# Layer 1's feed-forward block: the second product in smaller groups, five of eight row pairs by seven products, and two gate panels made as one double panel

## The chip, the cores and the metric

The kernel runs on one core of a Trainium2 chip. Its engines work side by side: TensorE (PE in the rows; PEld is its weight load) multiplies matrices, VectorE (DVE) and ScalarE (ACT) work element by element, GpSimd (POOL) does little here, and SyncE (SP) issues most transfers. Each engine takes its instructions in the order in which the program lists them for it. The metric is the time of one execution in microseconds (us) of device time, as the median of several runs.

## What is computed

Two layers in sequence on 256 tokens of width 2048, all in float32. Layer 1 is a mixer of two attentions with sigmoid gates, a cross attention to a memory, and a SwiGLU block; layer 2 is another gated mixer. Cut to what the change touches:

```python
def hybrid_mixer(x, ...):                       # layer 1
    o_a = dsa_attention(...)                    # 8 heads of 128
    o_b = moba_attention(...)                   # 8 heads of 128, causal with distance slopes at S = 256
    g_a = jax.nn.sigmoid(ga + b_gate[0])        # ga, gb: columns of x @ w_in
    g_b = jax.nn.sigmoid(gb + b_gate[1])
    merged = g_a * (o_a @ w_o_dsa) + g_b * (o_b @ w_o_moba)
    return merged @ w_out

def swiglu(x, w_in, w_out):                     # D_FF = 5632
    g, u = jnp.split(x @ w_in, 2, axis=-1)
    return (jax.nn.silu(g) * u) @ w_out

x = layer_norm(ALPHA * x + swiglu(x, w_ffn_in, w_ffn_out), ln_g[2], ln_b[2])
```

## The kernel before

**Products.** To keep float32 accuracy each operand is split into a rounded part `hi` (ScalarE, L107) and a remainder `lo` (VectorE, L108), and each product of two operands takes three matmuls: hi with hi, lo with hi, hi with lo (`mm3`, `mm3s`). The weights are the moving operand, 512 columns to a matmul. Weights come by DMA into `raw` tiles of 128x1024, which hold two blocks of 128 rows; there are six buffers each for `raw`, `hi` and `lo` (N_R, N_W). The 256 tokens are two halves, `tt` 0 and 1.

**Panels.** `gemm_panels` makes products of one panel (512 output columns) after another: per block of 128 rows 2 halves x 3 = 6 matmuls into two `ps_g` banks of PSUM. There are four `ps_g` banks and four `ps_m` banks.

**Double panels.** `duo` makes two panels together. It goes through the 16 row blocks in eight pairs. A pair in `eight` takes 2 blocks x 2 panels x 6 = 24 matmuls. A pair in `seven` takes seven block products of 3 matmuls in place of eight, 21 in all (Strassen's scheme in a variant): VectorE forms four sums of weight blocks (L255 one of 128x1024, L257 and L261 of 128x512 each), and these are split like weights, three tiles of 128x1024 and one of 128x512 in place of two tiles. L261 forms the last half of the tile that is split right after it. Sums of activations for a pair (`sums_of`) are made once per activation and kept. Four of the seven results gather in the four `ps_m` banks (`N`) over all pairs by seven; behind the last of them `combine` (L297 to L301) reads the banks, and the banks are free again. At the end `finish` (L305) adds each `ps_g` bank to the combined part, for (half, panel) in the order (0,0), (0,1), (1,0), (1,1). PLAN = (0, 3, 1, 4, 2, 5, 6, 7) is the order of the pairs, FAST = (0, 1, 2) those by seven.

**Queues of work.** `later_q` holds transposes of finished results, which `flush()` runs in the middle of a later product; `idle_q` holds small work of VectorE, of which `spare()` runs one piece between blocks. A scheduler then lists each engine's instructions in an order of its own within what the data allow.

**Around the change.** In the mixer, `ob = alibi_attention(...)` goes through four pairs of heads. For each, TensorE makes scores (L372), VectorE and ScalarE make the softmax, TensorE transposes the probabilities (L395, L396, L399), ScalarE copies them (L405), and TensorE weighs the values (L406, L407), all through `ps_m` banks. Next in the program stand the gate panels `ga[0]` and `ga[1]`, each a `gemm` of its own through `ps_g`, 96 matmuls each. Behind them stands `gate_pair` for `gb[0]`, `gb[1]`, a double panel.

In the feed-forward block `ffn_in(j)`, j = 0 to 10, makes 512 columns of g and of u (j = 0 as two single panels, the others as a double panel), `ev_g` applies silu, `ev_u` multiplies (L843), and `to_pair` transposes the result into `hT[j]` later. FFN_GROUPS cuts the second product: three `ffn_in` and the first of the next group, then four panels over 12 row blocks (288 matmuls); the last group has 8 row blocks. `residual` adds each panel of the second product to x (L721, L723).

Of the kernel before, what the change touches and what calls it, by code (L numbers as in the profile page):

```python
# [28 lines left out]
TAIL = 8  # L29
# [6 lines left out]
FAST2 = (0, 1)  # L36

FFN_GROUPS = ((0, 3), (3, 6), (6, 9), (9, 11))
# [6 lines left out]
def build(ctx, tc, nc, a):  # L45
# [167 lines left out]
    def duo(w0, w1, evacs, acts, sums, plan=PLAN, dest=None):  # L213
# [96 lines left out]
        rest, flushed = list(plan), False  # L310
        while rest:
            i = rest.pop(0)
            if i in sums:
                seven(i)
                if i == fast[-1]:
                    combine()
                    flush()
                    flushed = True
            elif len(rest) <= 1:
                eight([i] + rest)  # L320
                rest = []
            else:
                eight([i])
                if not fast and not flushed:
                    flush()
                    flushed = True
        return
# [350 lines left out]
    ga = {}  # L678
    ga[0] = gate_panel(a["w_ga"][0], xA, cols(0, 0), "ga")
    ga[1] = gate_panel(a["w_ga"][1], xA, cols(0, 1), "ga")  # L680
    gb = {}
# [149 lines left out]
    def ffn_in(j):  # L831
# [8 lines left out]
        hT[j] = pair("hT")  # L840

        def ev_u(tt, ps):
            nc.vector.tensor_mul(sg[tt], sg[tt], ps)  # L843
            later_q.append(lambda: to_pair(sg[tt], hT[j], tt))

        if j == 0:
            idle_q.extend(sums_later(x2S, x2T) + ln_affine(1))
            gemm(a["w_fi"][0], x2A, ev_g, head=HEAD)
            gemm(a["w_fi"][1], x2A, ev_u)
            spare(-1)  # L850
        else:
            duo(a["w_fi"][2 * j], a["w_fi"][2 * j + 1], (ev_g, ev_u), x2A, x2S, PLAN)
# [6 lines left out]

    groups = [range(j0, j1) for j0, j1 in FFN_GROUPS]  # L860
    for gi, g in enumerate(groups):
        for j in g:
            if j not in hT:
                ffn_in(j)
        last = gi == len(groups) - 1
        if not last:
            ffn_in(groups[gi + 1][0])
        flush()
        acts = acts_of([hT[q] for q in g])
        if last:  # L870
            hnT = [pair("hnT") for _ in range(4)]
            ln = layer_norm_T(g3[:, 0, :], g3[:, 1, :], hnT, None)
        gemm_panels([(a[f"w_fo{gi}"][j], acts, residual(j, gi == 0, last, ln)) for j in range(4)], tail=TAIL if last else 0)
# [349 lines left out]
```

## Time and profile before

| what | value |
|---|---|
| median of 3 runs | 2188.13 us (2187.45 to 2192.49) |
| the profiled execution | 2189.2 us |
| its span, first to last instruction | 2187.5 us |
| TensorE busy | 2163.9 us, 99% |
| VectorE busy | 1684.9 us, 77% |
| ScalarE busy | 1173.6 us, 54% |
| DMA | 426.10 MB, mean 195 GB/s |
| mean granted clock of TensorE | 0.999 |

Matmuls overlap in the pipeline, so that the time from one start to the next is their price, not the duration shown. The same holds for VectorE: the next instruction starts a little before the end that is shown.

### The profile page before, as it was taken

Reading aid. Unit: us, or ns where it says so; the run is one execution under the profiler, and the core shown is the slowest. Engines: PE = TensorE matmul, PEld = TensorE weight load, DVE = VectorE, ACT = ScalarE, POOL = GpSimd, SP = SyncE. Lnnn points to the kernel's source line nnn. Section 1 sums busy time; section 2 is a strip of 40 time slices with the busy share of each in tenths; the row PEclk is TensorE's granted clock in tenths of the full one; section 3 lists DMA queues with packets and bytes.
Section 4 is the critical chain, followed back from the end, with each engine's and each line's share of the span. In section 5 each row is a group of like instructions: output and inputs, shape, how many; then the busy total and the mean of one; then the engine's idle time right before and its main releaser. Section 6 shows DMA issues by size and latency. Waiting matters only on the chain.

```text
span 2187.5 us, 27170 instructions
## 1 busy us (share of the span) xinstructions
PE 2163.9 (99%) x9873; PEld 1780.2 (81%) x9873; DVE 1684.9 (77%) x2184; ACT 1173.6 (54%) x1494; POOL 43.2 (2%) x87
## 2 busy tenths in 40 slices
PE   8999999999999999999999999999999999999999
PEld 6888888888888788888888888877788787888887
DVE  5688877888767799858967886778676778998784
ACT  5665554455456555545544554547565656554542
POOL 1000000000000000000000000001000000000000
PEclk9999999999999999999999999999999999999999
DMA  7544646568666466655665665556645455665753
GB/s 280 180 154 136 225 135 206 183 202 270 207 206 212 140 202 216 207 190 174 198 227 170 204 208 185 202 182 227 208 158 179 162 193 178 220 204 182 247 201 129
DMA packets 138934, 426.10 MB, mean 195 GB/s; under 512 B 16000, under 2 KB 16560, under 8 KB 138800
## 3 DMA queue, kind: packets, MB, share of 16 engines
q1 hardware_dynamic: 132480, 403.40, 56.0%
q0 software_dynamic: 6320, 20.97, 3.0%
q8 instruction: 77, 1.26, 0.2%
q14 instruction: 57, 0.47, 0.1%
HBM read 420.11 MB, written 4.19 MB: 194 GB/s over the span
## 4 chain that ended last, share of the span: by engine, by line
PE 75%; issue 10%; DVE 8%; DMA 5%; ACT 2%; SPq 0%; POOL 0%; ACTq 0%; DVEq 0%; POOLq 0%
PE ps_g L132 11%; PE ps_g L131 11%; PE ps_g L130 11%; PE ps_g L211 10%; PE ps_g L210 10%; PE ps_g L209 10%; DVE lo L108 4%; PE ps_m L209 2%; PE ps_m L210 2%; PE ps_m L211 2%; DMA raw<-w_fi 1%; PE ps_t L339 1%; ACT hi L107 1%; DMA raw<-w_out 1%; DMA raw<-w_qkvg 1%
## 5 line engine op out<-in xcount | busy, mean ns | idle before, releaser
L107 ACT CAST hi<-raw 128x1024 fp32r<-128x1024 f32 (+1 forms) x904 | 905.4, 1016 | 864.5 <-PE ps_g L132 351.3
L108 DVE TENSOR_TENSOR lo<-raw,hi 128x1024 fp32r<-128x1024 f32 (+1 forms) x904 | 1048.2, 1174 | 362.6 <-ACT hi L107 354.9
L211 PE MATMUL ps_g<-hi,x2Tl 128*128 128x512 f32 x460 | 179.8, 391 | 0.0
L209 PE MATMUL ps_g<-hi,x2Th 128*128 128x512 f32 x460 | 179.8, 391 | 0.0
L210 PE MATMUL ps_g<-lo,x2Th 128*128 128x512 f32 x460 | 179.1, 389 | 0.0
L130 PE MATMUL ps_g<-hi,hTh 128*128 128x512 f32 x352 | 137.6, 391 | 0.0
L132 PE MATMUL ps_g<-hi,hTl 128*128 128x512 f32 x352 | 137.2, 390 | 0.0
L131 PE MATMUL ps_g<-lo,hTh 128*128 128x512 f32 x352 | 137.0, 389 | 0.0
L209 PE MATMUL ps_g<-hi,hnTh 128*128 128x512 f32 x334 | 130.4, 391 | 0.0
L211 PE MATMUL ps_g<-hi,hnTl 128*128 128x512 f32 x334 | 130.4, 390 | 0.0
L210 PE MATMUL ps_g<-lo,hnTh 128*128 128x512 f32 x334 | 130.4, 390 | 0.0
L132 PE MATMUL ps_g<-hi,hnTl 128*128 128x512 f32 x320 | 125.6, 393 | 1.3 <-DVE hnTl L759 1.3
L130 PE MATMUL ps_g<-hi,hnTh 128*128 128x512 f32 x320 | 126.4, 395 | 0.0
L131 PE MATMUL ps_g<-lo,hnTh 128*128 128x512 f32 x320 | 125.3, 391 | 1.0 <-DVE lo L108 1.0
L130 PE MATMUL ps_g<-hi,xTh 128*128 128x512 f32 (+1 forms) x288 | 114.1, 396 | 6.6 <-ACT hi L107 6.5
L255 DVE TENSOR_TENSOR raw<-raw 128x1024 f32<-128x1024 f32 x69 | 84.2, 1221 | 42.8 <-DMA raw<-w_qkvg 11.7
L131 PE MATMUL ps_g<-lo,xTh 128*128 128x512 f32 (+1 forms) x288 | 112.4, 390 | 0.8 <-DVE lo L108 0.8
L132 PE MATMUL ps_g<-hi,xTl 128*128 128x512 f32 (+1 forms) x288 | 112.7, 391 | 0.0
L211 PEld LDWEIGHTS ps_g<-hi,x2Tl 128*128 128x128 f32 x460 | 86.4, 188 | 18.0
L209 PEld LDWEIGHTS ps_g<-hi,x2Th 128*128 128x128 f32 x460 | 86.3, 188 | 17.7
L210 PEld LDWEIGHTS ps_g<-lo,x2Th 128*128 128x128 f32 x460 | 86.4, 188 | 17.6
L209 PE MATMUL ps_g<-hi,xTh 128*128 128x512 f32 x230 | 89.9, 391 | 0.0
(446 smaller groups left out, 4067.5 us busy)
## 6 DMA issues: line engine op xcount, KB each, us to landing
raw<-w_fi SPq DMA_DIRECT2D x116, 512.0 KB, 4.8
raw<-w_fo SPq DMA_DIRECT2D x88, 512.0 KB, 4.8
raw<-w_qkvg SPq DMA_DIRECT2D x82, 512.0 KB, 4.8
raw<-w_g SPq DMA_DIRECT2D x72, 512.0 KB, 4.9
raw<-w_fi SPq DMA_DIRECT2D x120, 256.0 KB, 4.0
raw<-w_out SPq DMA_DIRECT2D x54, 512.0 KB, 5.0
raw<-w_ga SPq DMA_DIRECT2D x26, 512.0 KB, 4.7
raw<-w_g SPq DMA_DIRECT2D x48, 256.0 KB, 3.9
```

What stands on the lines that cost most here:

```text
L107: nc.scalar.copy(hi, src)
L108: nc.vector.tensor_sub(lo, src, hi.bitcast(F32))
L130: nc.tensor.matmul(ps, ah[:, tok(tt)], wh, start=first, stop=False)
L131: nc.tensor.matmul(ps, ah[:, tok(tt)], wl, start=False, stop=False)
L132: nc.tensor.matmul(ps, al[:, tok(tt)], wh, start=False, stop=last)
L209: nc.tensor.matmul(ps, ah, wh, start=first, stop=False)
L210: nc.tensor.matmul(ps, ah, wl, start=False, stop=False)
L211: nc.tensor.matmul(ps, al, wh, start=False, stop=last)
L255: nc.vector.tensor_add(t13, ra, rb[:, 0:1, :].to_broadcast([128, 2, n]))
L339: nc.tensor.transpose(pt[:, i, :], src[:, i * 128:(i + 1) * 128], ident)
```

## The change

1. `ga[0]` and `ga[1]` become one double panel with pairs 0, 1, 2 by seven (PLAN).
2. In the feed-forward block the double panels of j = 2 to 10 take pairs 0 to 4 by seven, in the order 0, 5, 1, 2, 6, 3, 4, 7 (pairs 5, 6, 7 by eight). j = 1 keeps three. The sums of pairs 3 and 4 of this activation are made too.
3. FFN_GROUPS has six groups: `hT[0]` alone, and then two at a time. Behind each double panel from j = 1 on stand two of the four panels of the second product of an earlier group: 48 matmuls behind j = 1 and 2, 96 behind j = 3 to 10. The last group makes its four panels together at the end, as before. `hT` buffers are taken when they are written. There are 16 more additions to x.
4. `duo` calls `spare()` behind each pair by eight that isn't the last. The other edits in `duo` remove a flush that no call uses.

```diff
+PLAN5 = (0, 5, 1, 2, 6, 3, 4, 7)
+FAST5 = (0, 1, 2, 3, 4)
-FFN_GROUPS = ((0, 3), (3, 6), (6, 9), (9, 11))
+FFN_GROUPS = ((0, 1), (1, 3), (3, 5), (5, 7), (7, 9), (9, 11))
...
             else:
                 eight([i])
-                if not fast and not flushed:
-                    flush()
-                    flushed = True
+                spare()
...
-    ga[0] = gate_panel(a["w_ga"][0], xA, cols(0, 0), "ga")
-    ga[1] = gate_panel(a["w_ga"][1], xA, cols(0, 1), "ga")
+    ga[0], ga[1] = gate_pair(a["w_ga"][0], a["w_ga"][1], xA, xS, [cols(0, 0), cols(0, 1)])
...
         if j == 0:
-            idle_q.extend(sums_later(x2S, x2T) + ln_affine(1))
+            idle_q.extend(sums_later(x2S, x2T, FAST5) + ln_affine(1))
             gemm(a["w_fi"][0], x2A, ev_g, head=HEAD)
             gemm(a["w_fi"][1], x2A, ev_u)
+        elif j == 1:
+            duo(a["w_fi"][2], a["w_fi"][3], (ev_g, ev_u), x2A, {i: x2S[i] for i in FAST})
             spare(-1)
         else:
-            duo(a["w_fi"][2 * j], a["w_fi"][2 * j + 1], (ev_g, ev_u), x2A, x2S, PLAN)
+            duo(a["w_fi"][2 * j], a["w_fi"][2 * j + 1], (ev_g, ev_u), x2A, x2S, PLAN5)
...
-    groups = [range(j0, j1) for j0, j1 in FFN_GROUPS]
-    for gi, g in enumerate(groups):
-        for j in g:
-            if j not in hT:
-                ffn_in(j)
-        last = gi == len(groups) - 1
-        if not last:
-            ffn_in(groups[gi + 1][0])
-        flush()
-        acts = acts_of([hT[q] for q in g])
-        if last:
-            hnT = [pair("hnT") for _ in range(4)]
-            ln = layer_norm_T(g3[:, 0, :], g3[:, 1, :], hnT, None)
-        gemm_panels([(a[f"w_fo{gi}"][j], acts, residual(j, gi == 0, last, ln)) for j in range(4)], tail=TAIL if last else 0)
+    def ffn_out(gi, js, then=None, **kw):
+        acts = acts_of([hT[q] for q in range(*FFN_GROUPS[gi])])
+        gemm_panels([(a[f"w_fo{gi}"][j], acts, residual(j, gi == 0, then is not None, then)) for j in js], **kw)
+
+    for j in range(FFN_GROUPS[-1][1]):
+        ffn_in(j)
+        if j:
+            ffn_out((j - 1) // 2, ((2, 3), (0, 1))[j % 2])
+    hnT = [pair("hnT") for _ in range(4)]
+    ffn_out(len(FFN_GROUPS) - 1, range(4), layer_norm_T(g3[:, 0, :], g3[:, 1, :], hnT, None), tail=TAIL)
```

In the changed kernel's rows the lines up to 310 are two higher than before (L108 is L110, L255 is L257, L305 is L307), those of the attention two lower (L372 is L370), and the additions to x are L717 and L719.

**TensorE in the attention.** Before, in TensorE's order between the second and the third pair of heads: the values of a head are weighed (L406, L407), the last scores of the next pair follow (L372), and then eleven products of the gate panel (ps_g from xTh, xTl), of which the first three stand here, ahead of the next transpose (L395).

```order
L406 MATMUL ps_a<-pT,projV 128x256
L407 MATMUL ps_a<-pT,projV 128x128
L372 MATMUL ps_a<-projT 128x256
L130 MATMUL ps_g<-hi,xTh 128x512
L131 MATMUL ps_g<-lo,xTh 128x512
L132 MATMUL ps_g<-hi,xTl 128x512
```

In the changed kernel, at the same place:

```order
L404 MATMUL ps_a<-pT,projV 128x256
L405 MATMUL ps_a<-pT,projV 128x128
L370 MATMUL ps_a<-projT 128x256
L393 MATMUL ps_t<-ident,prob 128x128
L394 MATMUL ps_t<-ident,prob 128x128
L397 MATMUL ps_t<-ident,prob 128x128
L404 MATMUL ps_a<-pT,projV 128x256
```

The gate's products are gone from between the attention's. The first product into a `ps_m` bank stands behind the last transposes of the fourth pair of heads. From the first scores to there the list has 42 products of the gate panels, all ahead of the point where the second pair's values are weighed; before it has 104, through all four pairs.

**VectorE from a double panel to the second product.** Before, at the end of the double panel of j = 3 (L305 is `finish`, L843 the multiplication, the last three of L108's lo rows ahead of the fourth L305 belong to the second product):

```order
L305 TENSOR_TENSOR add<-add,ps_g 128x512 x2
L843 TENSOR_TENSOR sg<-sg,add 128x512
L108 TENSOR_TENSOR lo<-raw,hi 128x1024
L305 TENSOR_TENSOR add<-add,ps_g 128x512
L108 TENSOR_TENSOR lo<-raw,hi 128x1024 x2
L305 TENSOR_TENSOR add<-add,ps_g 128x512
L108 TENSOR_TENSOR hTl<-ps_t,hTh 128x4x128
L843 TENSOR_TENSOR sg<-sg,add 128x512
```

In the changed kernel, at the end of the double panel of j = 7 (j = 4 to 10 read alike):

```order
L302 TENSOR_TENSOR add<-add,ps_m 128x512
L307 TENSOR_TENSOR add<-add,ps_g 128x512
L303 TENSOR_TENSOR add<-ps_m,add 128x512
L837 TENSOR_TENSOR sg<-sg,add 128x512
L307 TENSOR_TENSOR add<-add,ps_g 128x512 x2
L110 TENSOR_TENSOR lo<-raw,hi 128x1024
L837 TENSOR_TENSOR sg<-sg,add 128x512
L110 TENSOR_TENSOR lo<-raw,hi 128x1024 x3
```

The first lo tile of the second product (L110, the first in these rows) now stands behind the last `finish`, and `combine` (L300 to L303) runs into `finish`.

**VectorE from the second product to the next double panel.** Before, where the last panel's addition to x (L721) is listed, behind lo tiles of the next double panel:

```order
L108 TENSOR_TENSOR lo<-raw,hi 128x1024 x2
L721 SCALAR_TENSOR_TENSOR x<-x,ps_g 128x512 x2
L108 TENSOR_TENSOR lo<-raw,hi 128x1024 x3
L255 TENSOR_TENSOR raw<-raw 128x1024
```

In the changed kernel (L719 adds the second of the two panels to x; the three lo tiles ahead of it are the last of pair 0 and the two of pair 5, and L257 belongs to pair 1):

```order
L110 TENSOR_TENSOR lo<-raw,hi 128x1024 x3
L719 TENSOR_TENSOR x<-x,ps_g 128x512 x2
L257 TENSOR_TENSOR raw<-raw 128x1024
L110 TENSOR_TENSOR lo<-raw,hi 128x1024
```

Nothing of pair 1 stands ahead of the end of the second product now.

## Rows read from the trace of the kernel before

**Rows 1.** The page: span, and busy time of each engine with its share.

```profile
span 2187.5 us, 27170 instructions
PE 2163.9 (99%) x9873; PEld 1780.2 (81%) x9873; DVE 1684.9 (77%) x2184; ACT 1173.6 (54%) x1494; POOL 43.2 (2%) x87
```

**Rows 2.** TensorE's waits: who for whom, us in total, times, longest.

```profile
PE ps_g L130 <- ACT hi L107: 6.5, 2, 5.4
PE ps_g L131 <- DVE lo L108: 1.8, 2, 1.0
```

**Rows 3.** Timeline of TensorE in the feed-forward block: start us, duration us, instruction.

```profile
899.64 0.39 PE L209 MATMUL ps_g<-hi,x2Th 128*128 128x512 f32 x1
...
904.86 0.39 PE L211 MATMUL ps_g<-hi,x2Tl 128*128 128x512 f32 x1
...
926.90 0.40 PE L211 MATMUL ps_g<-hi,x2Tl 128*128 128x512 f32 x1
927.14 0.60 PE L339 MATMUL ps_t<-ident,sg 128*128 128x128 f32 x4
927.49 0.48 PE L130 MATMUL ps_g<-hi,hTh 128*128 128x512 f32 x1
```

**Rows 4.** Timeline of TensorE around the second attention, the same columns.

```profile
285.26 1.47 PE L372 MATMUL ps_a<-projT 128*128 128x128 f32 x8
...
295.01 1.04 PE L372 MATMUL ps_a<-projT 128*128 128x128 f32 x6
...
313.11 1.04 PE L372 MATMUL ps_a<-projT 128*128 128x128 f32 x6
...
322.47 0.27 PE L399 MATMUL ps_t<-ident,prob 128*128 128x128 f32 x1
...
343.25 0.39 PE L209 MATMUL ps_m<-hi,xTh 128*128 128x512 f32 x1
```

**Rows 5.** Timeline of ScalarE and VectorE within one pair of heads.

```profile
298.46 0.67 DVE L383 TENSOR_REDUCE nmax<-prob 128x2 f32<-128x512 f32 x1
298.61 1.05 ACT L107 CAST hi<-raw 128x1024 fp32r<-128x1024 f32 x1 [0.50 <-ACT prob L386]
299.56 0.50 ACT L386 ACTIVATE prob<-prob,nmax 128x256 f32<-128x256 f32 x1
```

**Rows 6.** Timeline of VectorE over one pair by seven and one by eight.

```profile
802.31 1.22 DVE L255 TENSOR_TENSOR raw<-raw 128x1024 f32<-128x1024 f32 x1
803.44 1.21 DVE L108 TENSOR_TENSOR lo<-raw,hi 128x1024 fp32r<-128x1024 f32 x1
804.58 0.68 DVE L257 TENSOR_TENSOR raw<-raw 128x512 f32<-128x512 f32 x1
805.18 1.82 DVE L108 TENSOR_TENSOR lo<-raw,hi 128x1024 fp32r<-128x1024 f32 x2
806.92 0.68 DVE L261 TENSOR_TENSOR raw<-raw 128x512 f32<-128x512 f32 x1
808.77 3.50 DVE L108 TENSOR_TENSOR lo<-raw,hi 128x1024 fp32r<-128x1024 f32 x3 [1.18 <-ACT hi L107]
812.18 1.22 DVE L255 TENSOR_TENSOR raw<-raw 128x1024 f32<-128x1024 f32 x1
```

**Rows 7.** Timeline of VectorE at the end of a double panel before a second product.

```profile
926.12 2.35 DVE L108 TENSOR_TENSOR lo<-raw,hi 128x1024 fp32r<-128x1024 f32 x2
928.39 0.68 DVE L305 TENSOR_TENSOR add<-add,ps_g 128x512 f32<-128x512 f32 x1
```

**Rows 8.** Stretches: length, busy time by engine (instructions), granted clock, DMA share, GB/s.

```profile
285.20:323.40 38.20, 38.16 (x193) 30.71 (x193) 33.07 (x71) 23.90 (x54) 0.56 (x1) 1.00 0.42 138
760.00:770.00 10.00, 9.99 (x48) 7.80 (x47) 10.00 (x21) 10.00 (x21) 1.30 (x2) 1.00 0.25 83
```

**Rows 9.** Timeline of TensorE at the start of the kernel.

```profile
5.42 0.79 PE L130 MATMUL ps_g<-hi,xTh 128*128 128x512 f32 x1 [5.42 <-ACT hi L107]
...
7.16 0.63 PE L130 MATMUL ps_g<-hi,xTh 128*128 128x512 f32 x1
...
9.72 0.63 PE L130 MATMUL ps_g<-hi,xTh 128*128 128x512 f32 x1
10.15 0.46 PE L131 MATMUL ps_g<-lo,xTh 128*128 128x512 f32 x1
```

More of the change, by code (lines that the diff above doesn't have):

```diff
@@ L308, in finish @@
                 evacs[p](tt, P[tt][p])
-        rest, flushed = list(plan), False
+        rest = list(plan)
         while rest:
@@ L323, in duo @@
                 eight([i])
-                if not fast and not flushed:
-                    flush()
-                    flushed = True
-        return
+                spare()
     def acts_of(pairs):
@@ L676, in cols @@
         return a["b_gate"][0, row, j * 512:(j + 1) * 512]
-    ga = {}
-    ga[0] = gate_panel(a["w_ga"][0], xA, cols(0, 0), "ga")
-    ga[1] = gate_panel(a["w_ga"][1], xA, cols(0, 1), "ga")
-    gb = {}
+    ga, gb = {}, {}
+    ga[0], ga[1] = gate_pair(a["w_ga"][0], a["w_ga"][1], xA, xS, [cols(0, 0), cols(0, 1)])
     oaA, obA = acts_of(oa), acts_of(ob)
@@ L838, in ev_g, with turn @@
                 warm(AF.Sqrt, sg[tt][:, 511:512])
-        hT[j] = pair("hT")
         def ev_u(tt, ps):
             nc.vector.tensor_mul(sg[tt], sg[tt], ps)
-            later_q.append(lambda: to_pair(sg[tt], hT[j], tt))
+            def turn():
+                if j not in hT:
+                    hT[j] = pair("hT")
+                to_pair(sg[tt], hT[j], tt)
+            later_q.append(turn)
         if j == 0:
-            idle_q.extend(sums_later(x2S, x2T) + ln_affine(1))
+            idle_q.extend(sums_later(x2S, x2T, FAST5) + ln_affine(1))
             gemm(a["w_fi"][0], x2A, ev_g, head=HEAD)
             gemm(a["w_fi"][1], x2A, ev_u)
+        elif j == 1:
+            duo(a["w_fi"][2], a["w_fi"][3], (ev_g, ev_u), x2A, {i: x2S[i] for i in FAST})
             spare(-1)
         else:
-            duo(a["w_fi"][2 * j], a["w_fi"][2 * j + 1], (ev_g, ev_u), x2A, x2S, PLAN)
+            duo(a["w_fi"][2 * j], a["w_fi"][2 * j + 1], (ev_g, ev_u), x2A, x2S, PLAN5)
     g3 = const.tile([128, 2, 16], F32, name="g3")
```

## Prediction

> **What bounds the kernel now.** I read the page first: TensorE is busy for 99% of the span, VectorE for 77% [rows 1]. Busy time can hide gaps, since matmuls overlap, so next come TensorE's waits and its timeline. The longest entries of the waits are two that add up to 6.5 us, at the start of the kernel, and then 1.8 us [rows 2]: TensorE practically never waits. In the timeline the product at 899.64 and the 23rd after it at 904.86 lie 5.22 us apart, 0.227 us for each [rows 3]. So TensorE's own list is the bound, one product costs 0.227 us, and whatever makes TensorE wait is added to the time in full. The questions are how many products go, and whether TensorE still finds work at each point of its list. For the second I read how the lists of TensorE and VectorE stand against each other in the changed program, and took the length of each step from the trace.
>
> **Products removed.** A pair by seven takes 21 products in place of 24. The feed-forward block has 2 more such pairs in each of 9 double panels, 54 products fewer: 54 x 0.227 = 12.2 us. The gate panels have three, 9 products fewer, 2.0 us. The second product has the same 1056 products in all. Together 63 x 0.227 = 14.3 us, if nothing waits.
>
> The Trainium skill, page "TensorE: Matmul & The Clock Gate", section "Wait — 56ns, not 53.3ns?", gives 215.7 ns from start to start for 512 columns at 2.4 GHz; this trace shows 227 ns [rows 3], and the measurement decides. By the page's figure the 63 products would be worth an estimated 13.6 us.
>
> **The gate panels and the attention.** Before, TensorE makes the first scores of this attention at 285.26 and the last transposes at 322.47, 37.3 us later with their length; the pairs of heads follow each other some 9 us apart (three pairs from 285.26 to 313.11, 27.9 us) [rows 4]. That length is no work of TensorE's: it is the softmax that goes to and fro between VectorE and ScalarE. TensorE stays busy for 38.16 of 38.20 us there [rows 8] because 104 products of the two gate panels lie between. Now they form a double panel, and a pair by seven wants all four `ps_m` banks, which the attention uses to its end. Only what goes to `ps_g` can lie between: 9 products of pair 0, 24 of pair 3, 9 of pair 1, 42 in all; beyond that the six hi buffers are full of pairs 0 and 1. So TensorE stands still in the third and fourth pair of heads. What is gained in turn: fewer weight casts stand in the attention's way. One cast of 1.05 us at 298.61 keeps a softmax, whose maximum was ready at 299.13, until 299.56, some 0.4 us [rows 5]. With two such places in a pair of heads I take 0.8 us off three of the four, 2.3 us.
> From the first scores to the first product of the next double panel it takes 343.25 - 285.26 = 58.0 us before [rows 4]. After: 37.3 - 2.3 = 35.0 us to the last transposes, then the 183 - 42 = 141 products left, 32.0 us, and 0.6 us for the last weighing of values: 67.6 us. That is **9.6 us more**, the 9 products fewer included. Bounds: nothing off the attention, 12; two us off each pair of heads, 4.
>
> **VectorE within a double panel.** One pair by seven and one by eight take VectorE from 802.31 to 812.18, 9.87 us; a whole lo tile takes 1.14 us from start to start, a half one 0.60 [rows 6]. Two whole lo tiles off leaves 7.6 us for a pair by seven, with 1.18 us in which VectorE waits for ScalarE's cast of the tile that it has just summed; in the changed list nothing is put into this wait either. TensorE needs 21 x 0.227 = 4.8 us for it. A pair by eight takes VectorE 2.3 us, TensorE 5.4. With three by seven VectorE needs 3 x 7.6 + 5 x 2.3 = 34 us against TensorE's 41.5; with five 44.8 against 40.2, and the four steps of `combine`, four of `finish` and two multiplications come on top. The second product gives it back (eight lo tiles, 9 us, against 21.8), but only as far as buffers and the list let VectorE run ahead.
>
> **The handover to the second product.** I follow one round from TensorE's first product of a double panel (0). By VectorE's list the tiles of pairs 0 and 5 are ready; it must then wait for the last panel of the second product to add it to x, and is free at about 0.9. Pairs 1, 2, 6, 3, 4 take 4 x 7.6 + 2.3 = 32.7, the first tile of pair 7 1.1: 34.7. TensorE wants pair 4's last tile at 29.9 + 3.6 = 33.5, VectorE has it at 33.6: just in time. Now VectorE's list holds four steps of `combine`, four of `finish`, a multiplication (9 x 0.6 = 5.4) and the second tile of pair 7 (1.1): 41.2; only then comes the first lo tile of the second product, with its full 1.22: **42.4**. TensorE is through the double panel at 40.2, has two products that need no lo (0.45) and four transposes (0.35, from 927.14 to 927.49 [rows 3]), and waits from 41.0: **1.4 us**. Before, three lo tiles of the second product were made ahead of the last `finish` (two of them from 926.12 to 928.39 [rows 7]) and there was no wait. Even a VectorE that is never late cannot avoid it: the last `finish` can start only some 0.3 us after TensorE's last product has been issued, and 0.6 + 1.22 us later is 2.1, against TensorE's 0.8: 1.3 us. Nine rounds (j = 2 to 10) at 1.4 us: 12.6 us; at the floor 11.7.
> j = 3 is worse: the second product ahead of it has 48 products (10.9 us) in place of 96, and the addition to x stands in the middle of pair 0, with one half sum, the wait, and three lo tiles still to come: 0.6 + 1.2 + 3.4 = 5.2 us later than in the other rounds. j = 2 has one lo tile in this place, 1 us. I take 6 us for both (0 to 8).
>
> **Small things.** Two more sums of activations (two steps of half width and four of a quarter each, 2 us) fall where VectorE has no gap (10.00 of 10 us busy [rows 8]): 0 to 4 us, I take 2. The 16 more additions to x (0.6 us each) are one set per round, in the 0.9 above or beside the second product, where VectorE has time. Transfers move the same bytes; `hT` buffers and `spare` add no work.
>
> **The sum**, against the profiled execution of 2189.2 us: attention and gate panels +9.6, products of the feed-forward block -12.2, handovers +12.6, j = 2 and 3 +6, sums +2: +18.0, 2207.2. That execution lies 1.1 us above the median, so **2206 us**. With every term at its good end (4 - 12.2 + 11.7 + 0 + 0 = +3.5) 2192, at its bad end (12 - 12.2 + 9 x 2.5 + 8 + 4 = +34; 2.5 us a handover if a late transfer or cast costs VectorE 1 us a round) 2222.
>
> **Rivals.** (a) *The handover costs nothing, and the time is not slower than before.* Place: the first lo tile behind the last `finish`. If TensorE found its tile there, the block would keep its 12.2 us, which pays for the gate panels: 9.6 - 12.2 + 2 = -0.6, 2187.5. Below 0.1 us a handover the time is not longer, below 0.8 us the difference can't be measured. For it: VectorE has kept up with three pairs by seven throughout [rows 2]. Against it: the order of the list, which no speed of VectorE's changes. Chance 0.12.
> (b) *TensorE's clock falls while it stands still in the attention.* At the start of the kernel, after no work at all, the products from 7.16 to 9.72 lie 0.427 us apart, which is the level of 1.2 GHz, and from 10.15 on they go at 2.4 GHz [rows 9]; that start costs 11 products x 0.2 = 2.2 us. Once or twice that, and slower transposes within the chain of two pairs of heads: +4, 2210. Against it: the attention's own work goes on, and in the traced attention the granted clock is 1.00 [rows 8]. Chance 0.13.
> The Trainium skill, page "TensorE: Matmul & The Clock Gate", section "Part 1: The HAM clock gate", says that half rate is the default and activity releases it, which speaks against opening such a gap; rows 9 agree, but no run here shows an attention with gaps like these.
> (c) *VectorE sets the pace of every round.* Its chain of 42.4 us has no slack; if each pair by seven costs it 1 us more (a late transfer of the four pieces, a cast behind another), four of these add 4 us to each of 9 rounds, 36 us: 2242. Against it: the 9.87 us were measured with transfers running. Chance 0.05.
>
> **How the numbers follow.** Forecast 0.70, (a) 0.12, (b) 0.13, (c) 0.05. A measurement of this kernel tells about 0.3%, 6.6 us, from no change: 2181.6 to 2194.7. Faster has a part of (a) in which the attention also shortens by more than 6 us: 0.04. Within 0.3% are the rest of (a) and the good end of the forecast (0.04): 0.12. Slower 0.84. The range runs from 2194, the good end with something of each term, to 2224, (b) at the bad end; (a) and (c) lie outside.
>
> **What would show it.** Right: TensorE idle for some 15 us between 295 and 325 with the softmax as the releaser; idle of 1 to 2 us ahead of the first lo product of each second product, released by L110; a gate stage of about 67 us. Wrong: products of ps_m among the attention's, a TensorE without waits in the feed-forward block, or pairs of heads at 7 us.

## Result and profile after

| | us, median | range | 
|---|---|---|
| before, same runs | 2188.26 | 2187.45 to 2192.49 |
| after | 2221.11 | 2220.85 to 2223.61 |
| after : before | 1.0146 | 95% interval 1.0132 to 1.0161 |

The change is 32.9 us slower. That lies in the predicted range (2194 to 2224), near its upper end and 15 us above the predicted 2206. The profiled execution after took 2223.61 us, its span 2221.9 us, where before had 2189.2 and 2187.5.

The page of the kernel after: span and busy time of each engine with its share, as [rows 1] of before.

```profile
span 2221.9 us, 27298 instructions
PE 2171.0 (98%) x9810; PEld 1773.0 (80%) x9810; DVE 1781.1 (80%) x2325; ACT 1200.6 (54%) x1539; POOL 43.0 (2%) x87
```

The 63 products are gone, 9873 to 9810, worth 14.3 us, but the span grew by 34.4. VectorE's busy share rose by only three points.

TensorE's waits over the whole span after (who for whom: us in total, times, longest), some of them:

```profile
PE ps_g L133 <- DVE lo L110: 12.3, 12, 1.5
PE ps_t L393 <- DVE prob L377: 7.3, 5, 2.3
...
PE ps_m L212 <- DVE lo L110: 4.9, 8, 1.6
...
PE ps_t L394 <- DVE prob L377: 2.9, 4, 1.1
```

Before, the same product waited for lo tiles for 1.8 us (L131 in [rows 2]), and the transposes for the softmax:

```profile
PE ps_t L395 <- DVE prob L379: 1.7, 2, 0.9
```

Two places have grown. L133 and L212 wait for lo tiles, 11.0 and 3.2 us of it in the feed-forward block; L393 and L394, the transposes of the attention's weights, wait for the softmax. Laid side by side, the two traces put the loss in the same two places:

| stretch | before | after | more | forecast |
|---|---|---|---|---|
| first scores of layer 1's second attention to the first product of the next double panel | 285.26 to 343.25 | 285.37 to 360.75 | +17.4 | +9.6 |
| feed-forward block, first product with `x2T` to first product of layer 2 | 751.18 to 1468.72 (717.5) | 768.72 to 1502.71 (734.0) | +16.5 | +8.4 |

**The attention after.** TensorE's timeline (start, duration, instruction, idle time before it and its releaser), to be read against [rows 4]:

```profile
285.37 1.47 PE L370 MATMUL ps_a<-projT 128*128 128x128 f32 x8
...
294.80 1.04 PE L370 MATMUL ps_a<-projT 128*128 128x128 f32 x6
...
300.93 0.30 PE L393 MATMUL ps_t<-ident,prob 128*128 128x128 f32 x1 [1.38 <-DVE prob L377]
302.17 0.79 PE L212 MATMUL ps_g<-lo,xTh 128*128 128x512 f32 x1 [0.94 <-DVE lo L110]
...
306.52 1.91 PE L370 MATMUL ps_a<-projT 128*128 128x128 f32 x6
...
311.99 0.43 PE L393 MATMUL ps_t<-ident,prob 128*128 128x128 f32 x1 [2.32 <-DVE prob L377]
...
316.87 1.91 PE L370 MATMUL ps_a<-projT 128*128 128x128 f32 x6
...
326.95 0.42 PE L397 MATMUL ps_t<-ident,prob 128*128 128x128 f32 x1
327.02 0.77 PE L211 MATMUL ps_m<-hi,xTh 128*128 128x512 f32 x1
327.59 0.63 PE L212 MATMUL ps_m<-lo,xTh 128*128 128x512 f32 x1
328.02 0.63 PE L213 MATMUL ps_m<-hi,xTl 128*128 128x512 f32 x1
```

The same stretch in windows (length, busy time of PE, PEld, DVE, ACT and POOL with instructions, granted clock, DMA share, GB/s):

```profile
295.00:327.00 32.00, 21.07 (x79) 15.81 (x78) 19.48 (x51) 11.79 (x35) 0.00 (x0) 0.71 0.11 34
300.00:310.00 10.00, 7.18 (x24) 5.33 (x24) 6.71 (x18) 3.06 (x9) 0.00 (x0) 0.66 0.15 52
310.00:320.00 10.00, 6.29 (x22) 4.81 (x22) 4.65 (x16) 3.11 (x11) 0.00 (x0) 0.66 0.00 0
320.00:330.00 10.00, 6.05 (x20) 4.70 (x21) 3.35 (x10) 4.29 (x13) 0.00 (x0) 0.66 0.00 0
```

TensorE is idle for 10.9 of the first 32 us, and its granted clock falls to 0.66, a mean over stretches at 1.2 and at 2.4 GHz. The six score products that took 1.04 us take 1.91. The first products at 327.59 and 328.02 lie 0.43 us apart, the level of 1.2 GHz, as at the kernel's start [rows 9]. The last transposes end some 42 us after the first scores, where before took 37.3.

**The feed-forward block after.** The handover from a double panel to the second product, VectorE's timeline and then TensorE's:

```profile
1105.87 1.28 DVE L307 TENSOR_TENSOR add<-add,ps_g 128x512 f32<-128x512 f32 x2
1107.07 1.22 DVE L110 TENSOR_TENSOR lo<-raw,hi 128x1024 fp32r<-128x1024 f32 x1
```

```profile
1105.84 0.62 PE L132 MATMUL ps_g<-hi,hTh 128*128 128x512 f32 x2
1106.30 0.60 PE L337 MATMUL ps_t<-ident,sg 128*128 128x128 f32 x4
1108.34 0.50 PE L133 MATMUL ps_g<-lo,hTh 128*128 128x512 f32 x1 [1.44 <-DVE lo L110]
```

This is the predicted picture: two products, four transposes, then a wait for the first lo tile, which stands behind the last two `finish` steps. But a round, from one double panel's first product to the next one's (j = 4 to 10), takes 65.5 us on average. TensorE's own work in it is 177 + 96 products of 0.2267 us (24 in a row, from 334.19 to 339.63, take 5.44 us) and the hidden panel's transposes, 62.8 us (for the transposes 0.9 us: the second product of run e5, below, has no wait and takes 22.7 us, its 96 products 21.8). So 2.7 us are lost in each round, where 1.4 was forecast: 1.75 at the handover and in the second product, about 1 inside the double panel.

VectorE in about three such rounds after, first its busy time (third value behind the length), then all it waits for:

```profile
1000.00:1192.00 192.00, 186.53 (x824) 151.57 (x823) 169.78 (x192) 100.94 (x115) 0.00 (x0) 1.00 0.62 192
```

```profile
DVE lo L110 <- ACT hi L109: 16.5, 14, 1.2
DVE hTl L110 <- ACT hTh L109: 5.0, 3, 2.0
```

169.8 + 16.5 + 5.0 = 191.3 of 192 us. VectorE never waits for TensorE or for a transfer here. Its only waits are for ScalarE's cast of a tile that VectorE has just made itself, once in each pair by seven (the 1.18 us of [rows 6]), and of the hidden panel. With a busy share of 88%, VectorE's list as it stands leaves it no time. This was not in the prediction; the experiments test it.

### The profile page after: what moved, and what is told of

It reads as the page before. It is cut to its first block, busy times and chain, and to the rows that moved or that the text cites. A ratio compares the mean times of both kernels' runs of the same rounds, so it can differ in the third digit from the quotient of the medians.

```text
span 2221.9 us, 27298 instructions
## 1 busy us (share of the span) xinstructions
PE 2171.0 (98%) x9810; PEld 1773.0 (80%) x9810; DVE 1781.1 (80%) x2325; ACT 1200.6 (54%) x1539; POOL 43.0 (2%) x87
## 4 chain that ended last, share of the span: by engine, by line
PE 65%; DVE 21%; issue 5%; DMA 4%; ACT 4%; SPq 0%; ACTq 0%; DVEq 0%
DVE lo L110 11%; PE ps_g L134 10%; PE ps_g L133 10%; PE ps_g L132 10%; PE ps_g L212 8%; PE ps_g L211 8%; PE ps_g L213 8%; ACT hi L109 3%; DVE raw L257 2%; PE ps_m L211 2%; PE ps_m L212 2%; PE ps_m L213 2%; DMA raw<-w_fi 2%; PE ps_t L337 1%; DVE raw L259 1%
## 5 line engine op out<-in xcount | busy, mean ns | idle before, releaser
L110 DVE TENSOR_TENSOR lo<-raw,hi 128x1024 fp32r<-128x1024 f32 (+1 forms) x946 | 1082.0, 1165 | 307.1 <-ACT hi L109 301.2
L133 PE MATMUL ps_g<-lo,hTh 128*128 128x512 f32 x352 | 138.7, 394 | 11.0 <-DVE lo L110 11.0
L213 PE MATMUL ps_g<-hi,x2Tl 128*128 128x512 f32 x352 | 137.5, 391 | 0.0
L212 PE MATMUL ps_g<-lo,x2Th 128*128 128x512 f32 x352 | 137.5, 391 | 0.0
L211 PE MATMUL ps_g<-hi,x2Th 128*128 128x512 f32 x352 | 136.3, 392 | 0.6 <-ACT hi L109 0.6
L257 DVE TENSOR_TENSOR raw<-raw 128x1024 f32<-128x1024 f32 x90 | 109.8, 1221 | 29.3 <-DMA raw<-w_qkvg 9.8
L212 PE MATMUL ps_g<-lo,hnTh 128*128 128x512 f32 x334 | 130.6, 391 | 0.0
L133 PE MATMUL ps_g<-lo,hnTh 128*128 128x512 f32 x320 | 125.3, 391 | 0.4 <-DVE lo L110 0.4
L212 PE MATMUL ps_m<-lo,sums 128*128 128x512 f32 x270 | 107.6, 399 | 5.1 <-DVE lo L110 4.9
L212 PE MATMUL ps_g<-lo,xTh 128*128 128x512 f32 x276 | 107.8, 391 | 0.9 <-DVE lo L110 0.9
L213 PE MATMUL ps_g<-hi,xTl 128*128 128x512 f32 x276 | 108.2, 392 | 0.0
L211 PE MATMUL ps_m<-hi,sums 128*128 128x512 f32 x270 | 105.5, 397 | 1.8 <-ACT hi L109 1.7
L213 PE MATMUL ps_m<-hi,sums 128*128 128x512 f32 x270 | 105.6, 392 | 0.0
L132 PE MATMUL ps_g<-hi,xTh 128*128 128x512 f32 (+1 forms) x224 | 87.6, 391 | 6.4 <-ACT hi L109 6.2
```

The lines of the kernel that those rows point to most:

```text
L110: nc.vector.tensor_sub(lo, src, hi.bitcast(F32))
L132: nc.tensor.matmul(ps, ah[:, tok(tt)], wh, start=first, stop=False)
L133: nc.tensor.matmul(ps, ah[:, tok(tt)], wl, start=False, stop=False)
L211: nc.tensor.matmul(ps, ah, wh, start=first, stop=False)
L212: nc.tensor.matmul(ps, ah, wl, start=False, stop=False)
L213: nc.tensor.matmul(ps, al, wh, start=False, stop=last)
```

## Experiments

The difference is that from the kernel before, run on the same chip. The instructions behind the feed-forward block are the same in all, and from layer 2's first product to the last their traces take between 714.4 and 719.5 us. Differences below some 4 us between single kernels are therefore not read. e1, e3, e4 and e8 are edits of the kernel before and have its line numbers (e3's are one higher); the others are edits of the changed kernel.

| run | us | minus before, us | ratio, 95% interval |
|---|---|---|---|
| e1 gate pair alone | 2207.23 | +16.6 | 1.0067 to 1.0097 |
| e2 feed-forward part alone | 2208.47 | +17.9 | 1.0070 to 1.0103 |
| e3 gate pair, eights first | 2198.88 | +8.3 | 1.0023 to 1.0053 |
| e4 gate pair with useless products | 2203.53 | +12.9 | 1.0046 to 1.0076 |
| e5 three by seven, new order | 2187.43 | -3.8 | 0.9972 to 0.9992 |
| e6 four by seven | 2181.82 | -9.4 | 0.9944 to 0.9974 |
| e7 five, lo tiles ahead | 2205.17 | +13.9 | 1.0052 to 1.0082 |
| e8 both gate double panels reordered | 2191.63 | +0.4 | 0.9996 to 1.0014 |
| e9 five, group last | 2214.02 | +22.4 | 1.0085 to 1.0117 |
| e10 four, single last | 2182.63 | -9.0 | 0.9938 to 0.9971 |
| e11 e6 and e8 together | 2181.99 | -9.6 | 0.9940 to 0.9966 |
| e12 e6 again | 2182.07 | -9.5 | 0.9939 to 0.9965 |

**Where the loss sits.** e1 adds to the kernel before

```
+    ga, gb = {}, {}
+    ga[0], ga[1] = gate_pair(a["w_ga"][0], a["w_ga"][1], xA, xS, [cols(0, 0), cols(0, 1)])
```

and e2 takes the same lines out of the kernel after.

> The kernel before with one part of the change: layer 1's first two gate panels as a double panel, the feed-forward block as it was. Theory (the loss has two halves, about +17 us here and +16 us in the feed-forward block, as the two traces compare): 2205 us, 2203 to 2208; from the first scores to the first product of the output projections about 75 us, with the granted clock near 0.66 for some 30 us of it. Rival (the loss sits in the feed-forward block, and the attention stage only looks longer because work moved into it): 2186 to 2190 us.

> The changed kernel with its first two gate panels as two single panels again, so only the feed-forward part of the change is left. Theory: 2204.5 us, 2202 to 2207 (before plus 16.4), TensorE waiting 1 to 2 us at the first low-part product of each second product, and no stretch below clock 1.00 in the attention. Rival (the feed-forward part is about neutral, 12.2 us of products saved against 12 us of handovers): 2187 to 2191 us.

Measured: +16.6 and +17.9; together 34.5 against 32.9 for both. From the first scores to the first product of the memory projection e1 takes 377.4 us and e2 361.3 us, where before took 361.3. The feed-forward block takes 717.0 us in e1 and 735.2 in e2. The two halves are independent, as the theory had it (e2 lies 1.5 us above its range, beside a kernel before that ran 2.3 us slower than in the first runs). The rivals fall, and with them the idea that in this change the saved products pay for the waits.

**The gate pair: what fills the attention.** e3 is e1 with

```
+PLAN_GA = (3, 4, 5, 6, 0, 1, 2, 7)
-    ga[0], ga[1] = gate_pair(..., [cols(0, 0), cols(0, 1)])
+    ga[0], ga[1] = gate_pair(..., [cols(0, 0), cols(0, 1)], plan=PLAN_GA)
```

> The kernel before with the gate double panel, but the double panel takes its four row pairs by eight products ahead of the three by seven, so that what is open while the heads' softmax runs is eight-products, which need only a split. Theory (the loss of the gate pair is a lack of products ready between the heads, idle time and then the lower clock): about 2186 us (2183 to 2190): twelve products of 0.227 us saved more than the single panels had, 2.7 us, little else. Rival (a double panel there costs VectorE time that the softmax needs, wherever its row pairs stand): 2195 us or more, with TensorE still idle between the heads.

Measured +8.3: half of the loss is gone, not all. The theory's range is missed; the time is the rival's, but without the idle between the heads that the rival named. In the attention TensorE is nearly full (9.25 us or more of every 10 from 290 to 330) at clock 1.00. But TensorE now waits right behind it. TensorE's timeline of e3, where the next double panel begins, then VectorE's ahead of it:

```profile
343.22 0.39 PE L212 MATMUL ps_g<-hi,sums 128*128 128x512 f32 x1
345.04 0.50 PE L211 MATMUL ps_m<-lo,sums 128*128 128x512 f32 x1 [1.43 <-DVE lo L109]
```

```profile
341.96 1.28 DVE L668 TENSOR_TENSOR gp<-gp,bb 128x512 f32<-128x512 f32 x2
343.17 0.68 DVE L306 TENSOR_TENSOR gp<-gp,ps_g 128x512 f32<-128x512 f32 x1
343.77 1.22 DVE L109 TENSOR_TENSOR lo<-raw,hi 128x1024 fp32r<-128x1024 f32 x1
```

The last of the first double panel's `finish` steps (L306) and additions of the bias (L668) stand ahead of the lo tile that the next double panel's first pair by seven waits for. Up to the memory projection e3 takes 366.0 us, 4.7 more than before; the rest of its 8.3 is in the unchanged part behind, where its trace is the slowest of all (719.5). e8 therefore gives that next double panel an eight first:

```
-            gb[0], gb[1] = gate_pair(..., [cols(1, 0), cols(1, 1)])
+            gb[0], gb[1] = gate_pair(..., [cols(1, 0), cols(1, 1)], plan=(3, 0, 4, 1, 5, 2, 6, 7))
```

> The gate double panel with its row pairs by eight first, and the double panel behind it, of the next two gate panels, with an eight ahead of its first seven and a seven and an eight in turn. Theory (the 5 us of idle TensorE at the start of that second double panel, where seven's five VectorE steps stood behind the first one's combination, are what is left of the loss): 4 to 7 us faster than the run with the eights first alone, which is 1 to 4 us slower to 3 us faster than the kernel before on the same chip. Rival (VectorE's work there is too much in any order): within 2 us of that run.

Measured +0.4, 8 us less than e3, a little more than the theory's 4 to 7. The same stretch takes 361.8 us. TensorE's waits in e8 from 285 to 360, all of them:

```profile
PE ps_a L406 <- ACT pT L405: 0.6, 1, 0.6
PE ps_t L395 <- DVE prob L379: 0.3, 1, 0.3
PE ps_g L209 <- ACT hi L107: 0.2, 1, 0.2
```

The double panel as such costs nothing. What costs is that pairs by seven stand where the heads are open: their `ps_m` products cannot run there, and VectorE's work for them stands in the softmax's way (the rows are below, with the gate term). Its saving, three pairs of 3 products, 9 and not the twelve of the expectation, is worth 2.0 us and too small to be seen.

**The clock.** e4 is e1 with ten products of 512 columns in each pair of heads, written into the tile that the transposes then overwrite:

```
+            if i == 0 and busy:
+                for n in range(busy):
+                    nc.tensor.matmul(pt.rearrange("p a b -> p (a b)"), xT[n % 4][0][:, 0, 0:128],
+                                     xT[n % 4][0].rearrange("p a b -> p (a b)")[:, 0:512], start=True, stop=True)
```

> The kernel of the gate pair alone, with 10 extra products of 512 columns in each pair of heads, put into the tile that the transposes then overwrite: 40 products of no use, 9.1 us at full clock, where TensorE waits for the softmax. Theory that part of the loss is the clock: the granted clock stays near 1.00 through the attention, a pair of heads takes 8.3 to 9.1 us instead of 10.4 us, and the kernel is 4 to 8 us FASTER than the gate pair alone (2197 to 2201 us) in spite of the added work. Rival (all of it is waiting for VectorE, the clock costs nothing): no gain, within 1 us of the gate pair alone, or slower by up to 9 us.

Measured: 3.7 us faster than e1 with 9.1 us of useless work, a little under what the theory had asked for. Two pairs of heads follow each other after 9.05 and 10.1 us (first scores at 295.49, 304.54 and 314.68), in e1 after 11.4 and 9.3. From the first scores to the memory projection it takes 374.6 us against 377.4. Windows of e1, then of e4:

```profile
300.00:310.00 10.00, 6.14 (x24) 4.59 (x24) 7.48 (x19) 3.06 (x12) 0.00 (x0) 0.83 0.16 52
310.00:320.00 10.00, 5.66 (x23) 4.50 (x23) 5.19 (x17) 3.66 (x12) 0.00 (x0) 0.83 0.00 0
320.00:330.00 10.00, 8.33 (x30) 6.57 (x31) 2.83 (x7) 4.60 (x10) 0.00 (x0) 0.66 0.02 7
```

```profile
300.00:310.00 10.00, 10.00 (x52) 8.21 (x51) 8.30 (x17) 5.30 (x13) 0.00 (x0) 1.00 0.00 0
310.00:320.00 10.00, 7.99 (x35) 6.43 (x34) 5.98 (x18) 3.41 (x11) 0.00 (x0) 0.83 0.15 52
320.00:330.00 10.00, 8.12 (x39) 6.11 (x38) 4.86 (x10) 6.07 (x11) 0.00 (x0) 1.00 0.13 42
```

The clock is back in two of three stretches. The intervals of e1 and e4 overlap (1.0067 to 1.0076), so the 3 us are indicated by the medians and the two traces, not proved; they are the smaller part of the loss in any case. Nor is the clock all that differs: in e1 VectorE makes the sum of a pair by seven (L255) in the second pair of heads, at 297.72, in e4 only in the third, at 304.31, and in both kernels the pair of heads with the sum in it is the long one (11.4 and 10.1 us).

The clock's price is read better from pairs of heads in which VectorE has no work on weights. Length, busy times, clock as above, for the third pair of e1 and then the third of the kernel after, with the same instructions in each:

```profile
305.24:314.50 9.26, 5.14 (x23) 4.12 (x23) 4.94 (x15) 3.41 (x11) 0.00 (x0) 0.87 0.11 46
```

```profile
306.52:316.87 10.35, 6.35 (x23) 4.83 (x23) 4.94 (x15) 3.41 (x11) 0.00 (x0) 0.66 0.08 32
```

1.1 us more at 0.66 than at 0.87.

**The feed-forward block: regrouping or five by seven?** e5, e6, e9, e10 and e12 are e2 with other plans, e7 is e2 with one more edit. e5 and e6:

```
-PLAN5 = (0, 5, 1, 2, 6, 3, 4, 7)
-FAST5 = (0, 1, 2, 3, 4)
+PLAN5, FAST5 = (0, 3, 1, 4, 2, 5, 6, 7), (0, 1, 2)       # e5
+PLAN5, FAST5 = (0, 4, 1, 5, 2, 3, 6, 7), (0, 1, 2, 3)    # e6
```

> Layer 1's gate panels single as before; the feed-forward block in the changed kernel's new order (two panels of the second product behind each double panel), but with three row pairs by seven products and the order of the kernel before in each double panel, which ends with a group of two row pairs by eight. No product less than before. Theory (the loss of 17.9 us comes from five by seven, which leaves VectorE late at each handover, and not from the regrouping): within 3 us of the kernel before on the same chip, and no wait of over 0.5 us before the first low-part product of a second product. Rival (the handover itself costs 1.8 us, whatever runs ahead of it): 14 to 20 us slower than before.

> As the run with three, but four of eight row pairs by seven products, the last two row pairs still one group by eight: 3 products less in each of the nine double panels behind the second, 27 x 0.227 = 6.1 us of TensorE. Theory (it is the excess of VectorE's work over TensorE's time in a double panel, and its place ahead of the handover, that costs): 2 to 6 us FASTER than the kernel before on the same chip, stalls under 0.5 us a round. Rival (every step beyond three by seven overloads VectorE): stalls of over 1 us a round, 4 us or more slower than before.

Measured -3.8 and -9.4, both faster than their theories' ranges. The regrouping costs nothing, nor does the fourth pair: TensorE waits in no round, and e6 is faster than the kernel before. VectorE of e6 over the same 192 us as above, and its waits:

```profile
1000.00:1192.00 192.00, 192.00 (x858) 158.84 (x857) 166.93 (x184) 104.76 (x113) 0.00 (x0) 1.00 0.61 205
```

```profile
DVE lo L110 <- ACT hi L109: 12.1, 22, 1.2
DVE raw L257 <- DMA raw<-w_fi: 10.4, 9, 1.7
DVE add L307 <- PE ps_g L213: 1.2, 2, 0.6
```

VectorE's busy time is only 3 us less than with five, but it now waits 10.4 us for weights and 1.2 us for TensorE: it is ahead. That, not the busy share, tells four from five.

The lists differ in one thing more. VectorE in e6 from L263, the sum whose tile must go to ScalarE and back ([rows 6], L261 there):

```profile
1108.12 0.69 DVE L263 TENSOR_TENSOR raw<-raw 128x512 f32<-128x512 f32 x1
1108.72 2.35 DVE L110 TENSOR_TENSOR lo<-raw,hi 128x1024 fp32r<-128x1024 f32 x2
```

Here another lo tile stands in the wait. In these 192 us the wait of 1.2 us behind L263 comes in 14 of 14 pairs by seven in the kernel after, e2, e7 and e9, in none of 12 in e6 and in 3 of 12 in e10. With five by seven VectorE thus has more work and empty waits as well, and no run parts the two: its busy steps alone, 169.8 of 192 us, are 57.9 us a round, under TensorE's 62.8. Whether a list that fills these waits would carry five by seven was not tried.

**The wait's place or VectorE's round?** The kernel after and e6 differ in the number of pairs and in the order of the row pairs at the end. Three runs part these two. e7 keeps five by seven but lets `duo` load and split the second product's first four blocks between the `finish` steps of the first and the second 128 rows:

```
                     if used[tt][p] == total[tt][p]:
                         finish(tt, p)
+                if ahead and tt == 0 and not rest:
+                    ahead()
```

e9 keeps five and ends with the group of two, `PLAN5 = (0, 5, 1, 2, 3, 4, 6, 7)`. e10 takes four but ends with a single eight as the change does, `PLAN5 = (0, 4, 1, 5, 2, 6, 3, 7)`.

> The feed-forward part of the change, five by seven, as in the run of that part alone; but the first four low parts of the second product's weights are split ahead of the double panel's last two sums on VectorE, not behind them. Theory (the handover's 1.8 us is the first low part queued behind the combination): the wait before the first low-part product falls under 0.5 us, the wait inside the double panel of about 0.9 us a round stays, and the kernel is 11 to 16 us faster than that run, so 2 to 7 us slower than before. Rival (VectorE is late by the whole round, so that the wait only comes up elsewhere, at the hidden panel's transposes or in the next double panel): less than 5 us faster than that run.

> The feed-forward part of the change with five by seven, in another order: the double panel ends with the group of two row pairs by eight (order 0 5 1 2 3 4 6 7), so that 48 products, 10.9 us, run while VectorE combines. Theory order (what decides is what runs on TensorE behind the last seven): the second product takes 22.7 us, the double panel 41 to 42.5 us, and the kernel is 0 to 5 us slower than before on the same chip. Theory count (five by seven is more than VectorE can give in a double panel, in any order): the wait moves into the double panel, 43 us or more, and the kernel stays 9 us or more slower than before.

> Four by seven as in the fastest run so far, but with only one row pair by eight behind the last seven, as the change has it (order 0 4 1 5 2 6 3 7). Theory order: the handover's wait of 1 to 2 us a round comes back (second product 23.7 us or more), 8 to 16 us slower than the run of four with the group last. Theory count: within 3 us of that run, 6 to 11 us faster than before on the same chip.

| | double panel, us | second product, us | round, us | TensorE's own work, us |
|---|---|---|---|---|
| e5, three | 41.6 | 22.7 | 64.29 | 64.1 |
| e6, four, group last | 41.0 | 22.7 | 63.62 | 63.5 |
| e10, four, single last | 41.0 | 22.7 | 63.65 | 63.5 |
| e2, five, as in the change | 41.3 | 24.4 | 65.73 | 62.8 |
| e7, five, lo tiles ahead | 42.0 | 23.2 | 65.29 | 62.8 |
| e9, five, group last | 43.6 | 22.7 | 66.23 | 62.8 |

The rounds are means of six, from j = 4's first product to j = 10's. I had expected e7 to gain 11 to 16 us over e2; it gained 4, as its rival had it. In e9 the handover's wait is gone altogether, and the kernel is the slowest of all the feed-forward variants, since the wait has moved into the double panel. e10 has the change's order of row pairs at the handover and no wait. But its VectorE list is another one there:

```profile
1260.16 1.22 DVE L110 TENSOR_TENSOR lo<-raw,hi 128x1024 fp32r<-128x1024 f32 x1
...
1266.14 1.22 DVE L110 TENSOR_TENSOR lo<-raw,hi 128x1024 fp32r<-128x1024 f32 x1
```

TensorE's first lo product of the second product runs at 1265.56 without a wait, so its lo tile is the one at 1260.16 or an earlier one, and stands ahead of all four `finish` steps (1261.89 to 1265.54). e10 therefore shows that one pair by eight behind the last seven is enough; it does not test the change's list with four. With five the round takes 65.3 to 66.2 us in all three orders. VectorE of e9 in the same window:

```profile
1000.00:1192.00 192.00, 187.54 (x816) 149.12 (x815) 169.48 (x190) 101.59 (x114) 0.00 (x0) 1.00 0.59 193
```

```profile
DVE lo L110 <- ACT hi L109: 21.1, 17, 1.5
DVE add L307 <- PE ps_g L213: 0.9, 3, 0.3
```

169.5 + 21.1 + 0.9 = 191.5 of 192: full again. So theory "order" falls, by e7 and e9: with the lo tiles ahead of the handover the round is no shorter than 65.3 us. The handover is where VectorE's lateness shows, not what causes it. Theory "count" stands for the orders that were run; its "in any order" is not shown.

**Both parts repaired.** e11 takes e6's block and e8's two plans; e12 is e6 once more.

> Both repaired parts together: the feed-forward block with four by seven and the group last, and the gate double panel with its eights first and the one behind it with an eight first. Theory (the parts add: minus 9.5 us, and 0 to minus 2.7 us for twelve products less in the gate): 9 to 13 us faster than the kernel before on the same chip. Rival (the gate double panel costs in the attention what it saves, or pushes the stages behind it): less than 8 us faster, slower than the feed-forward part alone beside it.

> The run of four by seven with the group last once more, beside the one with both parts, on the same chip: 7 to 11 us faster than the kernel before if the first measurement holds; less than 5 us faster if it was the chip's luck.

Measured -9.6 and -9.5: the gain of e6 holds on a second chip, and the gate double panel adds nothing that can be told. e6, layer 1 as before, the second product in two panels behind each double panel and four by seven, beats both kernels: in e12 2182 us, a ratio of 0.9952 (0.9939 to 0.9965) to before.

## Why the prediction was right, and where its sum was off

**Direction and places: right.** Slower, in the gate panels and at the handovers. TensorE's idle time between the heads (forecast some 15 us, measured 10.9 between 295 and 327) is released by the softmax in all but one place (0.94 us, a lo tile of the weights), and no `ps_m` product stands among the attention's. The 1 to 2 us ahead of the first lo product are there, released by L110. e3 and e8 confirm the reason for the first: with eights in the attention, and an eight ahead in the next double panel, the loss is gone. That the sum fell into the range is in part luck: the gate term lies beyond its own bad end (12), and the range held because the feed-forward block stayed short of its own (-12.2 + 22.5 + 8 + 4 = 22.3).

**The gate term: +9.6 forecast, +17.4 measured.** The 42 products that fit between the heads and the 141 left for later were right. The mis-sized part is the softmax chain: 35.0 us to the last transposes, got by taking 2.3 us off the 37.3 for casts that no longer stand in the way. It took 41.6 us from the first scores to the start of the last transposes. The gain from the missing casts did not come, for two reasons. In the second pair of heads (11.7 us, before 9.1) VectorE's work for the pairs by seven stands in the softmax, which the step did not count:

```profile
298.71 1.22 DVE L257 TENSOR_TENSOR raw<-raw 128x1024 f32<-128x1024 f32 x1
...
299.92 0.67 DVE L381 TENSOR_REDUCE nmax<-prob 128x2 f32<-128x512 f32 x1
```

The maximum at 299.92 starts 5.1 us after this pair's first scores; before it was 3.45 (298.46 in [rows 5], 295.01 in [rows 4]). And at the lower clock TensorE's own transposes and scores became slower: the third and fourth pairs take 10.35 and 10.1 us, before 9.0 and 9.4, with no weights between. The tail was 1.2 us over (33.8 to 32.6), its first three products and a little more at 1.2 GHz. Rival (b) was not an alternative to the forecast but came on top of it, and I gave it 0.13 because the attention's own work goes on; that work did not hold the clock.

The Trainium skill, page "TensorE: Matmul & The Clock Gate", section "Part 1: The HAM clock gate", calls the lower rate the default that activity lifts. The traces of after and e4 agree: granted clock 0.66 with the gaps, 1.00 in most of the stretch with useless products in them.

**The feed-forward term: +8.4 forecast, +16.5 measured.** The 54 products, 12.2 us, went. The handover's wait was put at 1.4 us and measured up to 1.5; the second products took 24.4 us against 22.7 in e5, 1.75 more. What failed is the step that follows one round from a state in which VectorE is on time, and its result "just in time": it left out the wait inside the double panel, about 1 us a round, and the question whether VectorE can be on time at the start of every round. VectorE's round can be added up from the prediction's own numbers, the waits for ScalarE in each pair by seven included: five pairs by seven at 7.6 us and three by eight at 2.3 (44.9), ten half-width steps of `combine`, `finish` and multiplication (6.0), two lo tiles of the hidden panel (1.2), eight lo tiles of the second product at 1.14 (9.1), four additions to x (2.4): 63.6 us, and with the wait for the cast of the hidden panel (5.0 us in three rounds, 1.7 each) 65.3. TensorE's is 62.8. The measured round is 65.5. With four by seven the same sum gives 60.0 against 63.5, and less where the waits are filled; TensorE sets the pace in e6 and e10.

**Rival (c) had the mechanism and the wrong price.** "VectorE sets the pace of every round" is what happens, without the 1 us more per pair by seven that I had made its condition. Its price is not the 4 us a round that make 36 but the difference of the two rounds, 65.3 - 62.8 = 2.5 us. The forecast's range held the block's time because its handover (1.4 us, 2.5 at the bad end) was a part of the same lateness, counted under another name. The reason that it gave, the order of the list at the handover, explains where the wait stands and not the time: in e9 the lo tiles stand ahead, no wait is left there, and the kernel is slower; in e7 they stand ahead and the round is 0.4 us shorter. The floor of 1.3 us for a VectorE that is never late was not tested, since no run has the change's list and such a VectorE.

**j = 2 and 3.** Forecast 6 us, and two handovers of 1.4: 8.8. After, j = 3's double panel takes 46.3 us, 6.2 over TensorE's own 40.1, and the second product ahead of it 15.1 against 10.9; j = 2's double panel is 2.4 over and the second product behind j = 3 2.0. That is 14.8 us. With four by seven (e6 and e10 to e12) j = 3's double panel takes 41.9 to 42.7 and the second product ahead of it 10.9, so that most of this is VectorE's lateness as well, with 48 products too few to catch up. Some 1.5 us of the 15.1 are the clock: the granted clock is 0.66 from 915 to 920, products there lie 0.43 us apart, and in e2, where the clock stays at 1.00, the same second product takes 13.6. From j = 2 on TensorE loses 33.7 us in all (14.8, and 18.9 from j = 4 on), which less the 12.2 us of products is more than the 16.5 by which the blocks differ. The rest is time that before's block lost itself, 717.5 us against 3078 x 0.2267 + 11 x 0.9 = 708 for its products and transposes, which the forecast had taken for fixed; e5, with the same products in the new order, takes 714.3.

**Rival (a)**, a handover that costs nothing, is excluded by e2; no handover waits with one pair by seven less (e6, e10), where the list is another.

## What to carry to other kernels

Before giving TensorE's work to VectorE, add up VectorE's whole period, its forced waits for another engine included, and compare it with TensorE's; if it is longer, moving the work that is waited for only moves the wait, as in e7 and e9. An engine with a busy share of 88% can be full: look at what its remaining waits are for. Round trips to another engine are part of its period unless its list has other work to put into them, as in e6; waits for transfers or for TensorE are slack. Work that fills a latency chain must be of a kind that needs nothing the chain holds (banks, buffers, the other engines' queues); here the order of row pairs in two double panels decided 16 us (e1 and e8).

## What the hardware showed that was not expected

TensorE's clock fell in the attention with no listed wait between the heads longer than 2.32 us. TensorE's products stop at 299.5; until 302.17 it has one transpose, with waits of 1.38 and 0.94 us ahead of the two, and from there it runs at 1.2 GHz (the product at 302.76 takes 0.43 us to the next start). Behind that the granted clock is 0.66 in three stretches of 10 us, at both levels in turn. Ten useless products in each pair of heads gave 1.00, 0.83 and 1.00 in e4, where e1 has 0.83, 0.83 and 0.66, and made the kernel no slower.

The change of VectorE from late to early is sharp: with one pair by seven less, and the waits for ScalarE mostly filled, TensorE's loss goes from 2.7 us a round to 0.2 or less.
